# Thirteen of 31 back-substitution steps of the leaf inversions moved from GpSimd to VectorE

## The chip, the cores and the metric

One core of a Trainium2 chip runs the whole layer. The metric is the device time of one execution in microseconds (us). The kernel before takes 4035.48 us, the median of three runs (4032.93 to 4040.57). The engines are called as in the profile: PE (TensorE matmuls), PEld (its weight loads), DVE (VectorE), ACT (ScalarE), POOL (GpSimd) and SP (SyncE, whose queue issues all the DMAs).

## What is computed

An encoder layer over two sequences of 2048 and 256 tokens, 18 tiles of 128 tokens in all, in f32. A projection feeds two mixers side by side, a differential attention and a bidirectional RWKV7 recurrence; an output projection and a squared-ReLU MLP follow.

```python
z = jnp.einsum("bsd,dc->bsc", h, w_in)
o_da = diff_attn_mixer(z[..., :DA_COLS], ...)      # softmax(q k^T) of two halves, subtracted, times v
o_rw = rwkv7_mixer(z[..., DA_COLS:], ...)          # the scan below, in both directions
x = x + jnp.einsum("bsc,cd->bsd", mixed, w_out)
...
def step(state, inp):                               # rwkv7_scan, one token
    r_t, w_t, k_t, v_t, a_t, b_t = inp
    sa = jnp.einsum("dbhij,dbhj->dbhi", state, a_t)
    state = (state * w_t[..., None, :] + sa[..., :, None] * b_t[..., None, :]
             + v_t[..., :, None] * k_t[..., None, :])
    y = jnp.einsum("dbhij,dbhj->dbhi", state, r_t)
    return state, y
```

The kernel runs the scan in chunks of 64 tokens. Inside a chunk the recurrence is a triangular system of 64x64 for each head and direction, and its inverse is built from 32x32 diagonal blocks: each diagonal block is inverted by itself (the leaf), and a merge joins two of them.

## The kernel before, in words

Three stages follow one another: projection and preparation (to about 950 us of the trace), attention and recurrence together (about 950 to 2150 us), output projection and MLP (to the end).

In the middle stage the function `build` interleaves two streams of work in program order: `attn_stream`, which for each head and tile of 128 queries computes scores, exponentials and the product with the values, and `rw_units`, which goes through 18 units. A unit is one tile of the forward direction and one of the backward direction. For a unit numbered v the stream issues `rw_inter` for unit v+2 (products of the chunk, L933 to L942), `rw_leaf` for unit v+2, `rw_chain` for unit v (two chunks, one after the other, that carry the state S, L1043 to L1084) and `rw_merge` for unit v+1 (L973 to L1003). The order of the instructions on each engine is laid out when the kernel is built, by a planner that simulates a timeline and takes ready instructions by their place in the program; on the chip each engine then works through its own list in order.

The leaf works on 128 partitions that hold 64 diagonal blocks twice, each half for half of the columns. It loads the blocks (`lm`, L953, from the DRAM scratch MD that L942 writes) and the start value (`lx`, L954, unit columns), runs 31 back-substitution steps, and writes the result to the DRAM scratch XD (L963), from which the merge loads it (`xt`, L973). Each step is a multiply into `ltmp` and an add into `lx`; step i covers i rows and 16 - i // 2 columns. The tiles `lm`, `lx` and `ltmp` have one buffer each.

```python
for i in range(31, 0, -1):                                             # L955
    k0 = i // 2
    n = 16 - k0
    e = nc.vector if i >= LFV else nc.gpsimd                           # L958
    e.tensor_tensor(out=tmp[:, 0:i, 0:n], in0=lm[:, 0:i, i:i + 1].to_broadcast([128, i, n]),
                    in1=X[:, i:i + 1, k0:16].to_broadcast([128, i, n]), op=ALU.mult)
    e.tensor_tensor(out=X[:, 0:i, k0:16], in0=X[:, 0:i, k0:16], in1=tmp[:, 0:i, 0:n], op=ALU.add)
```

With LFV = 14 the steps 31 to 14 run on DVE and the steps 13 to 1 on POOL. In the same stage DVE also computes the row maxima of the attention scores (`nb`, L604, from PSUM), the sum of two exponential tiles (`P`, L639), the small combine steps (L617 to L626), the masks of the chunk products (L935) and the copies and state updates of the chain (L1043, L1044, L1051, L1072, L1073). POOL also copies `nat` into `tt` (L980) and computes small factors for the attention output (`ors`, L658 to L660). ACT takes the exponentials (L608, three score buffers `sc`), scales them (L631) and copies most PSUM results.

Of the kernel before, what the change touches and what calls it, by code (L numbers as in the profile page):

```python
# [57 lines left out]
class K:  # L58
# [886 lines left out]
    def rw_leaf(self, u):  # L945
# [9 lines left out]
# [5 lines that stand above are left out]
# [256 lines left out]
RUN0 = False  # L1216
HPS = ""
SCA = (0, 1, 2, 3)
LFV = 14
AT = 2  # L1220
XNB = 2
XTB = 2
# [94 lines left out]
```

## Time and profile before

| | |
|---|---|
| median of three runs | 4035.48 us (4032.93 to 4040.57) |
| the profiled execution | 4034.81 us, span of the trace 4032.6 us |
| busy over the span | PE 96%, DVE 61%, ACT 50%, POOL 14% |
| first and last leaf instruction | 996.2 us (DVE), 2087.4 us (POOL) |
| busy in the 1092 us from 996 to 2088 | PE 1045.54, DVE 844.41, ACT 832.67, POOL 322.12 us |

The shares over the whole span are an average over three stages; only the middle stage holds leaf work, so that its own stretch is the one to read. A group of instructions is listed with its line, its tiles (out<-in), its shape, its count, its busy time and mean duration, and the idle time of its engine just before it with what ended that.

### The profile page before, as it was taken

The numbers are of one execution on the slowest core, as the hardware profiler recorded it, in microseconds if no ns is written. First come the engines' busy times: TensorE is split into PE (matmuls) and PEld (weight loads), VectorE is DVE, ScalarE is ACT, GpSimd is POOL, SyncE is SP. The second block draws the span as 40 slices with busy tenths as digits, with TensorE's granted clock in tenths as the row PEclk, the third lists the DMA queues.
The fourth block names the chain that finished last, engine by engine and source line by source line (L and its number), as shares of the span: only waits on it lengthen the run. The fifth ranks groups of instructions, "written<-read, shape, count | busy, mean of one in ns | idle before, by whom it ended". The sixth has DMA issues, their size and how long they took to land.

```text
span 4032.6 us, 75020 instructions
## 1 busy us (share of the span) xinstructions
PE 3861.2 (96%) x28646; PEld 3444.1 (85%) x28646; DVE 2458.1 (61%) x5132; ACT 2033.0 (50%) x4652; POOL 568.6 (14%) x1062
## 2 busy tenths in 40 slices
PE   8999997887999999999998999999999999999999
PEld 7999997886787778777876889999999999999998
DVE  4245888866777878776875765444444444444443
ACT  4345666645777787777784234333333333333332
POOL 0000121111332223222323430000000000000000
PEclk9999997898999999999998999999999999999999
DMA  7566876774334435334324474222252222422221
GB/s 246 201 220 195 245 240 200 209 204 123 83 94 133 101 94 135 89 89 129 89 61 163 142 237 159 63 63 63 63 188 63 63 63 63 157 63 63 63 63 40
DMA packets 614583, 506.51 MB, mean 126 GB/s; under 512 B 250632, under 2 KB 543440, under 8 KB 607568
## 3 DMA queue, kind: packets, MB, share of 16 engines
q1 hardware_dynamic: 614224, 501.73, 42.2%
q8 instruction: 225, 3.69, 0.4%
q14 instruction: 134, 1.10, 0.1%
HBM read 336.41 MB, written 165.17 MB: 124 GB/s over the span
## 4 chain that ended last, share of the span: by engine, by line
PE 73%; DMA 9%; DVE 7%; ACT 5%; POOL 2%; SPq 2%; issue 2%; DVEq 0%; ACTq 0%; POOLq 0%
PE ups L100 7%; PE ups L101 7%; PE ups L102 7%; PE yps L102 7%; PE yps L101 7%; PE yps L100 7%; PE oo L650 4%; PE scp L933 3%; PE mm L100 3%; PE mm L102 3%; PE mm L101 3%; PE sc L601 2%; PE atp L645 2%; PE sc L602 2%; PE wops L100 2%
## 5 line engine op out<-in xcount | busy, mean ns | idle before, releaser
L517 DVE TENSOR_TENSOR acc<-yps,acc 128x512 f32<-128x512 f32 x576 | 392.0, 688 | 380.9 <-PE yps L102 380.9
L100 PE MATMUL ups<-h2hi,f_hi 128*128 128x384 f32 x1536 | 520.3, 339 | 0.0
L101 PE MATMUL ups<-h2lo,f_hi 128*128 128x384 f32 x1536 | 520.2, 339 | 0.0
L102 PE MATMUL ups<-h2hi,f_lo 128*128 128x384 f32 x1536 | 519.8, 338 | 0.0
L101 PE MATMUL yps<-f_lo,uh 128*128 128x512 f32 x1152 | 450.8, 392 | 0.0
L100 PE MATMUL yps<-f_hi,uh 128*128 128x512 f32 x1152 | 448.8, 390 | 0.0
L102 PE MATMUL yps<-f_hi,ul 128*128 128x512 f32 x1152 | 444.6, 393 | 0.0
L604 DVE TENSOR_REDUCE nb<-sc 128x1 f32<-128x512 f32 (+1 forms) x528 | 348.3, 676 | 130.8 <-PE sc L602 128.7
L137 ACT CAST f_hi<-f_raw 128x1024 fp32r<-128x1024 f32 x96 | 96.2, 1047 | 649.3 <-PE yps L102 647.6
L608 ACT ACTIVATE P<-sc,nb 128x512 f32<-128x512 f32 (+1 forms) x528 | 359.1, 684 | 82.6 <-DVE nb L604 80.0
L650 PE MATMUL oo<-vv,at 128*128 128x128 f32 x2080 | 303.9, 291 | 16.5 <-ACT at L647 13.4
L650 PEld LDWEIGHTS oo<-vv,at 128*128 128x128 f32 x2080 | 265.6, 198 | 40.9 <-ACT at L647 20.8
L505 DVE TENSOR_TENSOR ul<-u,uh 128x384 fp32r<-128x384 f32 x192 | 106.8, 556 | 307.4 <-ACT uh L504 303.7
L101 PEld LDWEIGHTS ups<-h2lo,f_hi 128*128 128x128 f32 x1536 | 288.2, 188 | 6.3
L100 PEld LDWEIGHTS ups<-h2hi,f_hi 128*128 128x128 f32 x1536 | 288.3, 188 | 5.9
L102 PEld LDWEIGHTS ups<-h2hi,f_lo 128*128 128x128 f32 x1536 | 288.2, 188 | 5.5
L100 PE MATMUL mm<-w_hi,hT_hi 128*128 128x256 f32 x864 | 259.8, 301 | 18.7 <-DVE qn L343 11.1
L601 PE MATMUL sc<-kt,qq 128*128 128x512 f32 (+1 forms) x528 | 246.1, 466 | 24.0 <-ACT P L608 17.0
L101 PE MATMUL mm<-w_lo,hT_hi 128*128 128x256 f32 x864 | 256.0, 297 | 0.2
L102 PEld LDWEIGHTS yps<-f_hi,ul 128*128 128x128 f32 x1152 | 216.1, 188 | 46.7
L102 PE MATMUL mm<-w_hi,hT_lo 128*128 128x256 f32 x864 | 255.5, 296 | 0.0
L142 ACT ACTIVATE f_hi<-f_raw,g 128x256 fp32r<-128x256 f32 x384 | 168.9, 500 | 171.2 <-PE ups L101 110.5
(237 smaller groups left out, 8713.2 us busy)
## 6 DMA issues: line engine op xcount, KB each, us to landing
f_raw<-w_ff SPq DMA_DIRECT2D x192, 256.0 KB, 2.9
f_raw<-w_ff SPq DMA_DIRECT2D x96, 512.0 KB, 4.4
AR<-aro SPq DMA_DIRECT2D x36, 512.0 KB, 3.9
qq<-QT SPq DMA_DIRECT2D x288, 64.0 KB, 2.4
ar<-AR SPq DMA_DIRECT2D x36, 512.0 KB, 4.9
bk<-BK SPq DMA_DIRECT2D x36, 512.0 KB, 3.8
ZT<-zs SPq DMA_DIRECT2D x84, 192.0 KB, 3.8
xt<-x SPq DMA_DIRECT2D x27, 512.0 KB, 4.5
```

Of the source, the lines that this page charges most:

```text
L100: mm(ps, lh, rh, start=start, stop=False)
L101: mm(ps, lh, rl, start=False, stop=False)
L102: mm(ps, ll, rh, start=False, stop=stop)
L137: nc.scalar.copy(hi[:, ks], raw)
L142: nc.scalar.activation(out=hi[:, k], in_=raw[:, k - k0], func=AF.Copy, scale=gk)
L505: nc.vector.tensor_tensor(out=ul[:, ns], in0=u2, in1=uh[:, ns].bitcast(F32), op=ALU.subtract)
L517: nc.vector.tensor_tensor(out=acc[j][:, cs], in0=ps, in1=acc[j][:, cs], op=ALU.add)
L601: nc.tensor.matmul(sc, qq[:, c, 0], kt, start=True, stop=False)
L604: nc.vector.tensor_reduce(out=m, in_=sc, axis=AX.X, op=ALU.max, negate=True)
L608: nc.scalar.activation(out=P, in_=sc, func=AF.Exp, bias=m, accum_out=(a["ls"][:, hf] if a["nh"] > 1 else a["l"])[:, c:c + 1])
L650: nc.tensor.matmul(a["op"], at[:, b], a["kv"][1][hf][:, b], start=k == 0, stop=k == a["n"] - 1)
L933: nc.tensor.matmul(ps[:, c], bk[hs, c, x].rearrange("p s t -> p (s t)"), ar[hs, c, x].rearrange("p s t -> p (s t)"), start=True, stop=True)
```

## The change

One constant is changed. It sets from which step on the leaf leaves DVE for POOL; with 1 all steps 31 to 1 run on DVE, and POOL has no leaf instruction left.

```diff
@@ -1216,7 +1216,7 @@
 RUN0 = False
 HPS = ""
 SCA = (0, 1, 2, 3)
-LFV = 14
+LFV = 1
 AT = 2
 XNB = 2
 XTB = 2
```

Per unit 26 instructions change their engine (13 multiplies, 13 adds), in 18 units 468. Nothing else in the program text differs, but the planner lays out all the lists of the program anew.

## Rows read from the trace of the kernel before

**Rows 1.** The page's busy times over the whole span: busy us, share of the span, instructions.

```profile
PE 3861.2 (96%) x28646; PEld 3444.1 (85%) x28646; DVE 2458.1 (61%) x5132; ACT 2033.0 (50%) x4652; POOL 568.6 (14%) x1062
```

**Rows 2.** Busy time of each engine in stretches of the middle stage (start:end, length, then busy us of each engine with instruction counts, granted TensorE clock, DMA share, GB/s): all the leaf work, then its first 400 us and the remainder.

```profile
996.00:2088.00 1092.00, 1045.54 (x12336) 862.85 (x12335) 844.41 (x2104) 832.67 (x2063) 322.12 (x821) 0.97 0.40 100
...
1000.00:1400.00 400.00, 375.44 (x4429) 314.67 (x4429) 307.51 (x793) 298.57 (x740) 120.30 (x309) 0.95 0.42 104
1400.00:2088.00 688.00, 666.10 (x7887) 544.75 (x7884) 533.17 (x1297) 531.41 (x1318) 201.55 (x511) 0.99 0.39 98
```

**Rows 3.** Groups of instructions of POOL in the stretch from 996 to 2088 us: the leaf's adds and multiplies.

```profile
L961 POOL TENSOR_TENSOR lx<-lx,ltmp 128x130 f32<-128x130 f32 (+12 forms) x234 | 94.0, 402 | 16.9
L959 POOL TENSOR_TENSOR ltmp<-lm,lx 128x130 f32<-128x130 f32 (+12 forms) x234 | 92.5, 395 | 39.0 <-DVE lx L961 22.6
```

**Rows 4.** Groups of DVE with different shapes kept apart, from 950 to 2260 us: leaf multiplies of shapes that the POOL steps have too, or nearly.

```profile
L959 DVE TENSOR_TENSOR ltmp<-lm,lx 128x133 f32<-128x133 f32 x18 | 5.2, 289 | 0.1
L959 DVE TENSOR_TENSOR ltmp<-lm,lx 128x110 f32<-128x110 f32 x18 | 5.0, 278 | 0.2
L959 DVE TENSOR_TENSOR ltmp<-lm,lx 128x120 f32<-128x120 f32 x18 | 5.0, 278 | 0.1
...
L959 DVE TENSOR_TENSOR ltmp<-lm,lx 128x96 f32<-128x96 f32 x18 | 4.5, 252 | 0.1
L959 DVE TENSOR_TENSOR ltmp<-lm,lx 128x78 f32<-128x78 f32 x18 | 4.4, 247 | 0.2
...
L959 DVE TENSOR_TENSOR ltmp<-lm,lx 128x56 f32<-128x56 f32 x18 | 4.1, 225 | 0.3
...
L959 DVE TENSOR_TENSOR ltmp<-lm,lx 128x30 f32<-128x30 f32 x18 | 3.9, 217 | 0.3
```

**Rows 5.** The groups of all DVE leaf instructions from 996 to 2088 us: adds and multiplies.

```profile
L961 DVE TENSOR_TENSOR lx<-lx,ltmp 128x31 f32<-128x31 f32 (+2 forms) x324 | 85.8, 265 | 4.5
L959 DVE TENSOR_TENSOR ltmp<-lm,lx 128x31 f32<-128x31 f32 (+2 forms) x324 | 85.7, 265 | 51.7 <-DMA lx<-eye 25.5 <-DMA lm<-MD 16.1 <-issue 3.9
```

**Rows 6.** Busy time in eight stretches in which POOL runs its 13 leaf steps, after 1470 us (columns as in rows 2; the first, the last, the sum).

```profile
1475.60:1488.20 12.60, 12.60 (x183) 10.36 (x178) 9.01 (x15) 9.78 (x26) 10.84 (x30) 1.00 0.20 51
...
2074.30:2087.60 13.30, 13.30 (x210) 10.79 (x210) 10.40 (x18) 12.37 (x32) 11.49 (x28) 1.00 0.21 50
sum 105.90, PE 105.90 PEld 87.08 DVE 83.23 ACT 86.26 POOL 90.12; mean PE 13.24 PEld 10.88 DVE 10.40 ACT 10.78 POOL 11.26
```

**Rows 7.** The same in six stretches in which DVE runs its 18 leaf steps.

```profile
1450.80:1472.60 21.80, 21.80 (x277) 18.17 (x278) 21.15 (x70) 18.85 (x47) 2.18 (x5) 1.00 0.36 104
...
2047.70:2074.20 26.50, 26.50 (x311) 21.28 (x310) 23.61 (x73) 20.55 (x53) 3.97 (x10) 1.00 0.17 46
sum 142.70, PE 138.26 PEld 114.56 DVE 133.13 ACT 106.90 POOL 20.05; mean PE 23.04 PEld 19.09 DVE 22.19 ACT 17.82 POOL 3.34
```

**Rows 8.** The same in seven stretches between two leaves, with no leaf step on either engine.

```profile
1488.20:1514.50 26.30, 25.58 (x276) 21.27 (x275) 19.20 (x41) 21.83 (x54) 3.35 (x8) 1.00 0.52 113
...
2018.70:2047.70 29.00, 27.59 (x283) 22.03 (x283) 20.90 (x45) 23.84 (x61) 3.03 (x9) 1.00 0.40 77
sum 202.30, PE 195.71 PEld 158.26 DVE 139.17 ACT 164.37 POOL 23.85; mean PE 27.96 PEld 22.61 DVE 19.88 ACT 23.48 POOL 3.41
```

**Rows 9.** Waits between 996 and 2088 us (who waited for whom: us in total, times, longest us).

```profile
ACT P L608 <- DVE nb L604: 68.9, 75, 5.2
...
ACT o L662 <- POOL ors L660: 13.6, 13, 2.8
...
PE sc L601 <- ACT P L608: 13.0, 9, 4.4
...
PE oo L650 <- ACT o L662: 1.7, 2, 0.9
```

**Rows 10.** The chain that ended last in the stretch from 1000 to 1400 us, by line.

```profile
by line: PE oo L650 13.3%; PE scp L933 12.1%; PE sc L601 6.9%; PE atp L645 6.2%; DMA XD<-lx 5.3%; PE sc L602 5.2%; POOL lx L961 4.5%; POOL ltmp L959 4.2%; ACT P L608 3.8%; issue 3.7%; PE bp L938 2.8%; DMA ar<-AR 2.4%; PE mp L987 2.1%; PE qp
```

**Rows 11.** SP's queue in order of time, first around 1150 us, then around 1560 us (start, us, queue, line, DMA, count): the write of a finished leaf, and the loads by its merge.

```profile
1148.62 2.60 SPq L963 DMA_DIRECT2D XD<-lx  x2
...
1154.58 0.36 SPq L954 DMA_DIRECT2D lx<-eye  x1
1154.99 2.78 SPq L973 DMA_DIRECT2D xt<-XD  x4
...
1551.76 1.95 SPq L963 DMA_DIRECT2D XD<-lx  x2
...
1569.80 2.06 SPq L973 DMA_DIRECT2D xt<-XD  x4
```

**Rows 12.** DVE in order of time inside one leaf (start, us, engine, line, instruction).

```profile
1453.52 0.23 DVE L959 TENSOR_TENSOR ltmp<-lm,lx 128x81 f32<-128x81 f32 x1
1453.79 0.24 DVE L961 TENSOR_TENSOR lx<-lx,ltmp 128x81 f32<-128x81 f32 x1
1454.07 0.24 DVE L959 TENSOR_TENSOR ltmp<-lm,lx 128x78 f32<-128x78 f32 x1
1454.34 0.24 DVE L961 TENSOR_TENSOR lx<-lx,ltmp 128x78 f32<-128x78 f32 x1
1454.50 0.69 DVE L604 TENSOR_REDUCE nb<-sc 128x1 f32<-128x512 f32 x1
1455.10 0.25 DVE L959 TENSOR_TENSOR ltmp<-lm,lx 128x100 f32<-128x100 f32 x1
```

**Rows 13.** Groups of DVE: the sum of two exponential tiles (both inputs in SBUF) in the stretch 2005.1:2018.7 (one of those of rows 6), in 1746.7:1779 (one of those of rows 8), and over 950 to 2260 us with shapes apart.

```profile
L639 DVE SCALAR_TENSOR_TENSOR P<-P,g,P 128x512 f32<-128x512 f32 x4 | 3.2, 848 | 0.0
...
L639 DVE SCALAR_TENSOR_TENSOR P<-P,g,P 128x512 f32<-128x512 f32 x8 | 5.7, 741 | 0.1
...
L639 DVE SCALAR_TENSOR_TENSOR P<-P,g,P 128x512 f32<-128x512 f32 x252 | 181.3, 765 | 2.9 <-ACT P L631 0.7
```

## The prediction

> **What bounds the kernel now.** I read the whole page first: PE is busy 96% of the span, DVE 61%, POOL 14% [rows 1]. That mean hides the stage that matters, so the next view is the busy time between 996 and 2088 us, where the leaf runs: PE 1045.54 of 1092 us, DVE 844.41 (77%), ACT 832.67 (76%), POOL 322.12 [rows 2]. PE is the bound there too, with 46 us of idle time, of which 25 us lie in the first 400 us, where the granted clock is also lower (0.95 against 0.99) [rows 2]. So what the change is worth is read from how long PE idles next to each kind of leaf work, and not from POOL's or DVE's busy time.
>
> The third view cuts the stage by what the leaf does. While POOL runs its 13 steps, PE is busy in all of 105.9 us and DVE in 83.23 (79%) [rows 6]. While DVE runs its 18 steps, DVE is busy in 133.13 of 142.7 us (93%) and PE in 138.26: 4.4 us idle, 3.1% [rows 7]. Between leaves DVE is at 69% and PE idles 6.6 of 202.3 us, 3.3% [rows 8]. The reader is to see that the POOL part is at present the one part of the unit in which PE never runs dry.
>
> **What leaves POOL.** 468 instructions with 94.0 + 92.5 = 186.5 us, 10.4 us per unit [rows 3]. None of that is PE's time. POOL's other work then no longer stands behind leaf steps: ACT waited 13.6 us for POOL's `ors`, and PE 1.7 us for what ACT did next [rows 9]. I book a gain of 1 us, between 0 and the 13.6.
>
> **What DVE takes on.** The 13 steps have 130, 120, 121, 110, 108, 96, 91, 78, 70, 56, 45, 30 and 16 elements. From the nearest DVE shapes [rows 4], 0.289 once, and two each of 0.278, 0.278, 0.252, 0.247, 0.225 and 0.217, gives 3.28 us for the multiplies; the adds cost the same (265 ns mean in both groups [rows 5]). That is 6.6 us per unit and 118 us in 18 units. DVE would stand at (844 + 118) / 1092 = 88%, still below PE: it doesn't become the bound by its sum.
>
> **What DVE gets back.** With POOL on the leaf, the sum of two tiles takes 848 ns on DVE, without it 741; over the stage the mean is 765, so 252 times 24 ns is 6 us [rows 13]. With the few other DVE instructions of the same kind I take 8 us in all, 0.4 us per unit, from the 118. The net load is 110 us, 6.1 per unit.
>
> The Trainium skill, page "SBUF — State Buffer", section "Who interferes with whom", says that a DVE instruction with two SBUF inputs and a GpSimd instruction that reads SBUF lock each other out, the later one blocking fully. That speaks for this change, and by it alone DVE could get back up to POOL's whole leaf time, 186 us, against 118 added, so DVE would end lighter and the terms below vanish. The trace agrees on the direction, with 848 against 741 ns [rows 13], and puts the size at a twentieth of that.
>
> **What lies on the path.** Three terms.
>
> First, the POOL part of a unit becomes more of the DVE part. A DVE step takes 142.7 / (6 x 18) = 1.32 us, since DVE alternates leaf instructions with others [rows 7, 12]; POOL's takes 105.9 / (8 x 13) = 1.02 [rows 6]. So 13.2 us with no PE idle become 17.2 us at 3.1%. The 4 extra us replace time between leaves, at 3.3%, and cost nothing. 13.2 x 3.1% is 0.41 us per unit, 7.4 us in all.
>
> Second, in those 13.2 us DVE has (105.9 - 83.2) / 8 = 2.8 us free [rows 6], and gets 6.1 more. 3.3 us per unit of its work, row maxima and sums among it, are done later, in a part where DVE is idle 31% [rows 8]. The trace of before shows no such backlog, so I bound it: 0, if the idle time takes all of it, and 18 x 3.3 = 59 us, if PE waits for all of it. Behind a late row maximum stands ACT's exponential (68.9 us of waits for L604 now), and behind that PE, which waits for a score buffer (13.0 us now) [rows 9]: about a fifth of ACT's wait reaches PE, and three score buffers take up the rest. I take a tenth, 6 us, since half of the late work is the leaf itself, which nobody awaits.
>
> Third, the leaf ends later by 4 us, or by up to 4 us earlier where the wait for the hand-over to POOL (22.6 us in all [rows 3]) falls away. After 1400 us this has a cover: the merge's load is issued 18 us after the leaf is written [rows 11], because it waits for the merge before. If that cover were gone the merge would be late, then the chain. Before 1400 us there is little: load of the next `lx`, then `xt`, 6.4 us behind the write in SP's queue [rows 11], and the POOL leaf stands on the chain that ended last with 8.7% of 400 us [rows 10]. What is late there is the recurrence, while attention fills PE; PE's idle share there is 6% [rows 2]. Seven units times 4 us at 6% is 1.7 us.
>
> No DMA is added or moved. The write of the leaf (L963) waits on DVE in place of POOL, and the score loads behind it in SP's queue wait with it; that is in the third term. No new wait stands on DVE: a step follows its predecessor on the same engine.
>
> Sum: 7.4 + 6 + 1.7 - 1 = 14 us. The profiled execution took 4034.81 us, 0.7 below the median of the three runs; 4034.8 + 14 = **4049 us**.
>
> **The rivals.** *The idle time takes it all.* DVE at 88% still has 130 us free, the leaf has nobody waiting for it after 1400 us, and PE's 3.1% in the DVE part might come from ACT and not from DVE, as the 3.3% without leaf work suggests [rows 7, 8]. Then the first two terms are nothing and the time is 4036 us, within 8 us of before. For it speaks that both idle shares agree; against it, that PE idles nothing in the POOL parts.
>
> *The leaf gets shorter, and the kernel faster.* A DVE step whose two instructions follow each other takes 0.54 us [rows 12] against POOL's 1.02. If the planner puts the last 13 steps back to back, the leaf ends 13 x 0.48 = 6 us earlier, plus 1.3 us for the hand-over. In the early units that stand on the chain [rows 10], the recurrence then gains 7 x 7 = 50 us of lead, and could feed PE where it idles: at most the 25 us in the first 400 us [rows 2]; I take half, 12 us, which gives 4022 us. It needs steps that aren't alternated with other work; the DVE steps of now mostly are.
>
> By the skill's rule above, with DVE lighter than before, the time would also come out here, at or below 4035 us; 24 ns against 741 [rows 13] leave that little weight, and its chance is in that of this rival.
>
> *DVE becomes what PE waits for.* From the point at which the work put off in one leaf isn't done before the next begins, PE waits for row maxima in every unit. 3.3 us put off meet 8.9 us of free DVE time between leaves (63 us in seven stretches [rows 8]), of which the longer leaf takes 4 us of length. The price is up to the 59 us above, with the first term 66, so about 4100 us at the end and 4075 in the middle. Against it speaks the margin.
>
> **How the numbers follow.** The forecast, a small loss of 5 to 25 us (4040 to 4060): 0.40. All absorbed, 4028 to 4043: 0.27. Faster, 4010 to 4027: 0.18. DVE as the bound, 4060 to 4100: 0.15. A measurement of this kernel can tell about 0.2%, 8 us, so same means 4027 to 4043.5. Faster is the third case, 0.18; same is the second and a little of the forecast, 0.32; slower is the remaining 0.50. The range leaves out the lower half of the third case and the upper third of the last: 4020 to 4085. The forecast's own range is 4040 to 4060.
>
> **What would show it.** In the changed trace L959 and L961 stand on DVE with 558 instructions each and together near 290 us (171.5 + 118), and on POOL with none. DVE is busy 945 to 965 us of the leaf's stretch. L639's mean falls from 765 to about 741. A leaf takes about 41 us from its first step to its last, in one alternating run on DVE. PE's idle time in the stage grows by 10 to 15 us, in the places where POOL worked, with DVE's L604 ahead of it in the waits. The first step is wrong if PE stays fully busy in the leaf's last 13 steps; the second if ACT's wait for L604 doesn't grow from 68.9 us; the third if merges after 1400 us wait for the leaf. The prediction as a whole is wrong if the planner lays out PE's list so differently that the stage moves by more than these terms, or if the time is below 4027 us.

## The result and the profile after

The changed kernel takes 4055.24 us, the median of six runs (4051.02 to 4065.62), against 4036.79 for the kernel before (six runs, 4022.96 to 4040.57): a ratio of 1.0053, 95% interval 1.0040 to 1.0066, that is 18.5 us slower by the medians and 21 by the ratio. The forecast was 14 us, 4049 us. The profiled execution of the changed kernel is the longest of its six (4065.62 us, 10 us over their median), so what its trace shows against [rows 1 to 13] adds up to 31 us and not to 18.5.

The page's busy times (as rows 1):

```profile
PE 3865.8 (95%) x28646; PEld 3459.5 (85%) x28646; DVE 2526.8 (62%) x5600; ACT 2036.5 (50%) x4652; POOL 389.8 (10%) x594
```

The same number of matmuls; 468 instructions have gone from POOL to DVE. The busy time by stretches (as rows 2); the fourth line goes from 950 us to the first matmul of the output projection:

```profile
996.00:2088.00 1092.00, 1033.40 (x12112) 865.62 (x12111) 887.86 (x2489) 822.47 (x2031) 146.21 (x346) 0.95 0.40 99
...
1000.00:1400.00 400.00, 371.52 (x4280) 314.85 (x4279) 329.27 (x935) 303.72 (x747) 53.56 (x129) 0.94 0.40 97
1400.00:2088.00 688.00, 657.88 (x7810) 547.34 (x7807) 556.99 (x1551) 515.28 (x1277) 92.65 (x217) 0.95 0.40 100
...
950.00:2198.90 1248.90, 1156.94 (x13606) 969.08 (x13605) 977.92 (x2721) 916.51 (x2260) 177.24 (x409) 0.94 0.41 101
```

For the last line the kernel before has this one:

```profile
950.00:2170.00 1220.00, 1149.01 (x13592) 949.65 (x13592) 909.78 (x2242) 912.57 (x2257) 344.35 (x873) 0.96 0.41 103
```

The stage is 28.9 us longer, which is nearly all of the 31 us. PE's idle time grew from 71.0 to 92.0 us, and its busy time for the same work by 7.9 us at a granted clock of 0.94 in place of 0.96. The loss lies after 1400 us more than before it: there the clock was 0.99 [rows 2] and is 0.95. The last copy of a chain product ends the recurrence; before and after (minimum, median, maximum ns, first and last start):

```profile
L1051 DVE COPY q<-qp x36: 649/682/693, 1075.7 to 2149.7; 128x512 f32<-128x512 f32 x36
```

```profile
L1051 DVE COPY q<-qp x36: 675/688/693, 1091.0 to 2185.8; 128x512 f32<-128x512 f32 x36
```

The recurrence starts 15 us later and ends 36 us later. In all 14 traces of this case the first matmul of the output projection follows the last of these copies after 13 to 23 us, so that the end of the recurrence dates the end of the stage.

**The leaf on DVE.** Groups of DVE from 996 to 2150 us (as rows 5), then the sum of two exponential tiles over 950 to 2260 us (as rows 13):

```profile
L959 DVE TENSOR_TENSOR ltmp<-lm,lx 128x126 f32<-128x126 f32 (+22 forms) x558 | 142.5, 255 | 58.2 <-DMA lx<-eye 34.0 <-DMA xt<-XD 16.2 <-DMA qq<-QT 2.3
L961 DVE TENSOR_TENSOR lx<-lx,ltmp 128x126 f32<-128x126 f32 (+22 forms) x558 | 142.4, 255 | 6.6 <-DVE l L621 0.2
```

```profile
L639 DVE SCALAR_TENSOR_TENSOR P<-P,g,P 128x512 f32<-128x512 f32 x252 | 180.0, 761 | 1.6 <-ACT P L631 0.7
```

The leaf's instructions add up to 284.9 us on DVE, 113 more than in [rows 5], but DVE's busy time in the stage grew by only 68 us (909.78 to 977.92 above) and between 996 and 2088 us by 43 (844.41 to 887.86, where 945 to 965 was forecast). Over the whole trace DVE's instructions last 118.7 us longer in sum and its busy time grew by 68.7: neighbouring instructions overlap in the records, and 50 us of what was added lies in such overlaps.

DVE in order of time: the first and last instruction of one leaf, and the first of the next (start, us; in brackets the idle time before and what ended it):

```profile
1494.69 0.21 DVE L959 TENSOR_TENSOR ltmp<-lm,lx 128x31 f32<-128x31 f32 x1 [3.79 <-DMA xt<-XD]
...
1548.45 0.18 DVE L961 TENSOR_TENSOR lx<-lx,ltmp 128x16 f32<-128x16 f32 x1
...
1562.71 0.21 DVE L959 TENSOR_TENSOR ltmp<-lm,lx 128x31 f32<-128x31 f32 x1 [4.15 <-DMA xt<-XD]
```

From the first start to the last this leaf takes 53.8 us, and the next begins 14.3 us later. Read so for all 18 units, the mean length is 52.8 us (before: 40.5), and 17 times out of 17 the next leaf follows after 9 to 15 us (before: 9 to 15 us behind the first seven leaves, 24 to 34 us from then on). From one leaf's start to the next it is 64.3 us in the mean, 61.8 before. SP's queue between these two leaves (as rows 11):

```profile
1549.75 3.77 SPq L963 DMA_DIRECT2D XD<-lx  x2
...
1558.70 0.53 SPq L954 DMA_DIRECT2D lx<-eye  x1
1559.28 2.36 SPq L973 DMA_DIRECT2D xt<-XD  x4
```

The one buffer of `lx` takes its new start value only after the write, and the first merge's load goes out 9.5 us after the write (5.9 to 11.0 in the later units), where before it went out 18 us after it in [rows 11] (8 to 28 in the later units): the merge now always waits for the leaf.

**Where PE idles.** The unit cut up as in rows 6 to 8, after 1400 us: sums over 11 stretches with the first 18 steps, 12 with the last 13 steps, 11 between leaves.

```profile
sum 377.75, PE 352.59 PEld 293.22 DVE 325.20 ACT 297.73 POOL 71.56; mean PE 32.05 PEld 26.66 DVE 29.56 ACT 27.07 POOL 6.51
...
sum 232.16, PE 228.19 PEld 189.48 DVE 211.25 ACT 180.06 POOL 19.85; mean PE 19.02 PEld 15.79 DVE 17.60 ACT 15.01 POOL 1.65
...
sum 129.77, PE 122.22 PEld 102.45 DVE 64.70 ACT 82.88 POOL 9.34; mean PE 11.11 PEld 9.31 DVE 5.88 ACT 7.53 POOL 0.85
```

PE is idle 6.7% of the first 18 steps (3.1% in [rows 7]), 1.7% of the last 13 (nothing in [rows 6]) and 5.8% between leaves (3.3% in [rows 8]); over all units after 1400 us, cut as here, the kernel before has 3.9, 0.9 and 3.8%. Over all 18 units, the first 18 steps and then the last 13, before:

```profile
sum 488.30, PE 463.02 PEld 383.09 DVE 443.25 ACT 373.15 POOL 79.76; mean PE 25.72 PEld 21.28 DVE 24.62 ACT 20.73 POOL 4.43
...
sum 245.60, PE 242.40 PEld 201.16 DVE 181.94 ACT 187.13 POOL 202.06; mean PE 13.47 PEld 11.18 DVE 10.11 ACT 10.40 POOL 11.23
```

And after:

```profile
sum 601.30, PE 558.52 PEld 467.18 DVE 514.74 ACT 471.01 POOL 108.04; mean PE 31.03 PEld 25.95 DVE 28.60 ACT 26.17 POOL 6.00
...
sum 353.00, PE 343.11 PEld 287.97 DVE 326.05 ACT 274.00 POOL 30.49; mean PE 19.06 PEld 16.00 DVE 18.11 ACT 15.22 POOL 1.69
```

PE's idle time in the last 13 steps grew by 6.7 us (3.2 to 9.9), and in the first 18 by 17.5 (25.3 to 42.8); between leaves it fell by 5.5 (18.0 to 12.5). So most of it came not where the steps came in but in the first part of the next leaf, where the merge now falls. One such place in four-microsecond windows, with PE's two waits in it and the two of ACT ahead of them:

```profile
1492.00:1496.00 4.00, 3.78 (x22) 2.73 (x21) 1.17 (x4) 0.00 (x0) 0.00 (x0) 1.00 0.71 171
1496.00:1500.00 4.00, 0.72 (x33) 0.62 (x33) 3.26 (x9) 1.64 (x6) 2.40 (x6) 0.91 0.40 108
1500.00:1504.00 4.00, 4.00 (x18) 3.88 (x18) 2.96 (x9) 3.93 (x10) 0.00 (x0) 0.50 0.30 75
...
1516.00:1520.00 4.00, 4.00 (x33) 3.61 (x32) 3.19 (x8) 1.39 (x5) 1.96 (x4) 0.96 0.73 231
```

```profile
1497.13 0.69 PE L987 MATMUL mp<-zt,sc 32*32 32x32 f32 x32 [1.35 <-DVE zt L981]
...
1499.97 2.07 PE L650 MATMUL oo<-vv,at 128*128 128x128 f32 x8 [2.14 <-ACT o L662]
```

```profile
1496.14 0.46 ACT L976 COPY nat<-xt 128x256 f32<-128x256 f32 x1 [5.22 <-DMA xt<-XD]
...
1499.55 0.37 ACT L662 ACTIVATE o<-oo,ors 128x128 f32<-128x128 f32 x1 [2.20 <-POOL ors L660]
```

ACT's list stands 5.22 us at the merge's copy `nat`, which waits for the load of the finished leaf. PE then waits for the merge's `zt` and for the attention output `o`, is busy 0.72 of 4 us, and runs fully busy at a granted clock of 0.50 (1.2 GHz) from 1500 until about 1516. Three microseconds of waiting cost more behind them, in a stretch that counts as busy. This is an example and not the sum: between 996 and 2100 us PE's waits for `zt` are 1.4 us in all and ACT's for `xt` no longer than before (46.3 us, before 49.3). What grew most is PE's wait for ACT's exponentials.

Waits from 996 to 2100 us (as rows 9):

```profile
ACT P L608 <- DVE nb L604: 67.9, 61, 4.2
ACT nat L976 <- DMA xt<-XD: 46.3, 18, 5.2
...
PE sc L601 <- ACT P L608: 22.5, 14, 3.8
```

In [rows 9] the first is 68.9 us and the last 13.0.

### The profile page after: what moved, and what is told of

It reads as the page before. It is cut to its first block, busy times and chain, and to the rows that moved or that the text cites. A ratio compares the mean times of both kernels' runs of the same rounds, so it can differ in the third digit from the quotient of the medians.

```text
span 4063.8 us, 74972 instructions
## 1 busy us (share of the span) xinstructions
PE 3865.8 (95%) x28646; PEld 3459.5 (85%) x28646; DVE 2526.8 (62%) x5600; ACT 2036.5 (50%) x4652; POOL 389.8 (10%) x594
## 5 line engine op out<-in xcount | busy, mean ns | idle before, releaser
L604 DVE TENSOR_REDUCE nb<-sc 128x1 f32<-128x512 f32 (+1 forms) x528 | 350.6, 677 | 105.5 <-PE sc L602 102.9
L650 PE MATMUL oo<-vv,at 128*128 128x128 f32 x2080 | 307.2, 293 | 24.4 <-ACT at L647 13.7
L143 DVE SCALAR_TENSOR_TENSOR f_lo<-f_raw,g,f_hi 128x256 fp32r<-128x256 f32 x384 | 168.7, 482 | 139.7 <-ACT f_hi L142 137.3
```

Source lines behind the costliest of these rows:

```text
L143: nc.vector.scalar_tensor_tensor(out=lo[:, k], in0=raw[:, k - k0], scalar=gk, in1=hi[:, k].bitcast(F32), op0=ALU.mult, op1=ALU.subtract)
L604: nc.vector.tensor_reduce(out=m, in_=sc, axis=AX.X, op=ALU.max, negate=True)
L650: nc.tensor.matmul(a["op"], at[:, b], a["kv"][1][hf][:, b], start=k == 0, stop=k == a["n"] - 1)
```

## The experiments

Three theories. **A, length:** the leaf, now 53 us with some 10 us of reload behind it, sets the pace of the recurrence. **B, load:** the 26 more instructions per unit hold up DVE's other work, whatever the leaf's length. **C, POOL:** what POOL loses gives time back, because its list is no longer held by leaf steps (C1) or because it no longer gets in DVE's way in SBUF (C2). Every kernel was timed in turn with the kernel before, whose median stands in brackets. Costs in us are ratios, or differences of ratios, times 4036, and their uncertainty is that of the two intervals together.

**Load without length.** The kernel before, with 26 further DVE instructions per unit of the shapes of steps 13 to 1. In the first kernel they read the leaf's own `lm` and `lx`:

```diff
+for i in range(13, 0, -1):
+    n = 16 - i // 2
+    nc.vector.tensor_tensor(out=self.dt[:, 0:i, 0:n], in0=lm[:, 0:i, i:i + 1]..., in1=X[:, 13:14, 8:9]..., op=ALU.mult)
+    nc.vector.tensor_tensor(out=self.dx[:, 0:i, 0:n], in0=self.dx[:, 0:i, 0:n], in1=self.dt[:, 0:i, 0:n], op=ALU.add)
```

> The kernel before, with the 26 DVE instructions of steps 13 to 1 added per unit on two tiles that nobody reads, while POOL still runs the real steps; the output is that of before. Theory A (the leaf's length: 53 us from first step to last in the changed trace against 41 before, and the next leaf can start only when the last one has been written): DVE gets the load but the leaf keeps its length, so 0 to 8 us slower than the kernel before. Theory B (the 118 us of DVE work make row maxima late and PE idle): the whole loss is here, 15 to 20 us slower.

4053.28 us [4036.28], ratio 1.0041 (1.0025 to 1.0057), leaf 41.2 us. But the gap between leaves grew to 15 to 21 us in the first ten units, since the added instructions keep `lm` and `lx` in use. The second kernel frees them: only the first added instruction reads the leaf, and the others use tiles of their own.

```diff
+    src = X[:, 13:14, 8:9] if i == 13 else self.dx[:, 0:1, 0:1]
+    nc.vector.tensor_tensor(out=self.dt[:, 0:i, 0:n], in0=self.dc[:, 0:i, 0:n], in1=src.to_broadcast([128, i, n]), op=ALU.mult)
+    nc.vector.tensor_tensor(out=self.dx[:, 0:i, 0:n], in0=self.dc[:, 0:i, 0:n], in1=self.dt[:, 0:i, 0:n], op=ALU.add)
```

> The kernel before with the 26 extra DVE instructions per unit on tiles of their own; unlike the first run of this kind they read neither lm nor, but once, lx, so that they can't hold the leaf's buffers. Theory A: 0 to 8 us slower than before, the first run's 17 us having come from buffers held. Theory B: 15 to 20 us slower again.

4051.61 us [4033.46], 1.0036 (1.0022 to 1.0050), leaf 41.7 us, gaps of 10 to 15 us in the first seven units and 18 to 35 us later, nearly as before. DVE's load alone costs 15 to 17 us (uncertainty 6) with the leaf's length nearly unchanged. B holds, and A alone doesn't explain the change. In the second kernel part of this price goes another way than in the changed kernel, where POOL has no leaf steps: POOL's `ors` [rows 9] comes later, ACT's wait for it grew from 13.6 to 35.4 us and PE's behind it from 1.7 to 11.6. In the changed kernel the two are 7.7 and 2.7 us.

**Two buffers for `lm`, `lx` and `ltmp`**, in the changed kernel and in the kernel before, so that a leaf can start while the last one is being written:

```diff
-        X = sp.tile([128, 32, 16], F32, name="lx", tag="lx", bufs=1)
+        X = sp.tile([128, 32, 16], F32, name="lx", tag="lx", bufs=2)
```

> The changed kernel with two buffers each for lm, lx and ltmp in place of one, so that a leaf may be loaded and begun before the previous one has been written. Theory A: most of the 18 us of loss goes, 4030 to 4042 us. Theory B: the DVE load is the same, 4050 to 4060 us.

> The kernel before with two buffers each for lm, lx and ltmp. Theory A: the early units, where one leaf follows straight on another, speed up, 4 to 12 us faster than before. Theory B: nothing changes on DVE, within 4 us of before. It is also the partner of the run with two buffers and all steps on DVE: the difference of the two is the price of the DVE load without the serial leaf, near 0 to 6 us under A, 15 or more under B.

The changed kernel: 4041.90 us [4036.28], 1.0015 (1.0004 to 1.0025). The leaf is still 51.5 us long, but the first two leaves and the fifth overlap with the next, the mean from one start to the next is 61.8 us again, and the recurrence ends where it did before:

```profile
L1051 DVE COPY q<-qp x36: 679/685/692, 1097.9 to 2151.6; 128x512 f32<-128x512 f32 x36
```

With all of DVE's load kept, 15 us of the 21 are gone (0.0015 in place of 0.0053, uncertainty 7 us): a long leaf costs where the next must wait for it. The kernel before: 4038.24 us [4036.28], 1.0007 (0.9997 to 1.0018); A's gain did not come, so at 40.5 us the wait for the buffers does not set the time. The two kernels with two buffers differ by 0.0008, 3 us with an uncertainty of 6, which is what A gave for the pair. That doesn't make the load free: the pair also differs by the POOL work that the changed kernel no longer has, and the runs below price it.

**Steps 13 to 1 left out**, then their load put back beside the leaf, on POOL or on DVE:

```diff
-        for i in range(31, 0, -1):
+        for i in range(31, 13, -1):
```

> The kernel before with the 13 POOL steps left out (steps 13 to 1 aren't computed at all, so the inverses are incomplete): the leaf is some 14 us shorter, DVE's list of work is as before. Theory A, if the leaf's length sets the pace of the recurrence in the kernel before too: 8 to 20 us faster than before. Theory B: POOL's work is off the path, within 4 us of before.

> The same 18-step leaf with the 26 instructions per unit on DVE instead: the DVE load of the change with a leaf 14 us shorter than that of before. Theory A: 4003 to 4012 us. Theory B (the DVE load is what costs): 4018 to 4025 us, 15 to 20 above the 18-step leaf.

> The 18-step leaf (steps 13 to 1 left out, as in the earlier run at 4003 us), and 26 POOL instructions of the shapes of the left-out steps per unit on tiles that nobody reads, begun when step 14 is done: POOL's load of before without its place in the leaf. Theory A (the leaf's length set the 33 us that leaving the steps out gained): 4003 to 4010 us. Theory C (POOL's leaf work itself slows DVE or holds POOL's other work): 4025 to 4036 us.

Without the steps 4002.84 us [4036.28], 0.9919 (0.9905 to 0.9934), 33 us, more than either theory gave. With the DVE load of the kernel above 4020.69 us [4033.46], 0.9964 (0.9947 to 0.9981). With the same instructions on POOL 4028.96 us [4033.46], 0.9985 (0.9970 to 0.9999). Beside the first, the DVE load costs 0.0045, 18 us with an uncertainty of 9, a third time about the same; and the POOL load costs 0.0066, 27 us with an uncertainty of 8, although nobody waits for it: C holds, and POOL's leaf work was far from free. With POOL's load kept, the shorter leaf by itself gained 6 us (0.9985, uncertainty 6). The kernel with the DVE load differs from the changed kernel only in that steps 13 to 1 are off the leaf's chain: 0.9964 against 1.0053, 36 us with an uncertainty of 9. That is A, at a leaf of 25.8 us in the one and 52.8 in the other.

**POOL held without reading SBUF.** The same short leaf, with one small POOL instruction that waits for the leaf and 25 memsets, to tell C1 from C2:

```diff
+        nc.gpsimd.tensor_tensor(out=self.dx[:, 0:1], in0=self.dc, in1=X[:, 13, 8:9], op=ALU.mult)
+        for i in range(25):
+            nc.gpsimd.memset(self.dx[:, 0:400], 0.0)
```

> The 18-step leaf (steps 13 to 1 left out) and, in place of the 26 POOL instructions with two inputs, one small POOL multiply and 25 POOL memsets of 128x400 per unit on a tile that nobody reads: POOL is held for about as long, but the memsets read nothing. Theory C1 (POOL's leaf work costs because its other work stands behind it in its list): about as slow as with the two-input instructions, 4020 to 4035 us. Theory C2 (it costs because two-input instructions on POOL and DVE hold each other): 4003 to 4012 us, as the 18-step leaf alone.

4022.26 us [4035.77], 0.9964 (0.9951 to 0.9976). Its memsets, and its sum of two exponential tiles:

```profile
L966 POOL MEMSET dx<- 128x400 f32 x450 | 196.4, 436 | 23.4
```

```profile
L639 DVE SCALAR_TENSOR_TENSOR P<-P,g,P 128x512 f32<-128x512 f32 x252 | 178.9, 754 | 4.5 <-ACT P L631 2.6
```

Holding POOL for 196 us costs 0.0045 beside the short leaf, 18 us, with DVE undisturbed (754 ns; 757 with no POOL load, 777 with the two-input load). So most of C is not C2: what two-input instructions add, 0.0021 or 8 us, is no larger than its uncertainty. That it is C1 is what remains of the two, and this trace does not show the wait that carries it: ACT's wait for POOL's `ors` is 11.4 us, with the short leaf alone 10.7.

**The whole leaf on POOL** (`LFV = 32`):

> The opposite change: all 31 steps on POOL (the constant at 32). DVE loses 171 us of work. A POOL step takes about 1 us, so the leaf would be near 33 us long against 41 before. Theory A: 5 to 20 us faster than before. Theory B, by DVE's load: 10 to 25 us faster too. Theory C: POOL's doubled leaf work holds its other work and DVE, no gain or slower.

4076.41 us [4033.46], 1.0104 (1.0079 to 1.0128), with the shortest leaf (34.7 us) and 127 us less of DVE (717.93 against 844.41 us from 996 to 2088). By A and by B it should have gained. Here the waits show C1:

```profile
ACT o L662 <- POOL ors L660: 78.2, 37, 4.5
...
PE oo L650 <- ACT o L662: 24.4, 17, 2.6
```

Against [rows 9], ACT waits 78.2 us in place of 13.6 for POOL's `ors`, behind leaf steps in POOL's list, and PE waits 24.4 in place of 1.7 us for ACT.

**A longer leaf without load.** The kernel before with three round trips of `lx` through DRAM between steps 14 and 13:

```diff
+            if i == 13:
+                for z in range(3):
+                    nc.sync.dma_start(out=self.LD[u % 4], in_=X)
+                    nc.sync.dma_start(out=X, in_=self.LD[u % 4])
```

> The kernel before with three round trips of lx to DRAM and back put between the last DVE step and the first POOL step, so that the leaf gets some 12 us longer and no engine but the DMA queue gets more work; results as before. Theory A (a leaf of 53 us and 10 us of reload set the pace of the recurrence): 15 to 30 us slower than before. Theory B (DVE's load is the whole loss): within 5 us of before.

4116.46 us [4035.77], 1.0193 (1.0169 to 1.0216). The leaf takes 57.5 us and the next follows after 9 to 12 us in all 17 cases; the reload stands behind the write as in the changed kernel:

```profile
1664.00 2.57 SPq L968 DMA_DIRECT2D XD<-lx  x2
...
1669.97 0.35 SPq L955 DMA_DIRECT2D lx<-eye  x1
...
1671.49 2.07 SPq L978 DMA_DIRECT2D xt<-XD  x4
```

```profile
996.00:2088.00 1092.00, 985.20 (x11577) 832.19 (x11578) 782.06 (x1962) 785.76 (x1936) 290.63 (x750) 0.94 0.46 120
```

78 us for 17 us per unit, 306 us in 18 units. That is far above the 15 to 30 us that A gave, and it came with a lighter DVE (782 us), so B does not hold here. But the run has not only the length: its round trips go through the one DMA queue and hold POOL's list, and two waits that are not the leaf's show it:

```profile
ACT o L662 <- POOL ors L660: 39.8, 23, 4.5
PE scp L934 <- DMA ar<-AR: 31.1, 11, 4.1
```

Before, they are 13.6 us [rows 9] and 3.7 us, and the DMA share is 0.46 against 0.40. How much of the 78 us is the length alone is not shown.

**Other splits** (`LFV = 8` and `LFV = 5`):

> The kernel before with the constant at 8: steps 13 to 8 move to DVE, 7 to 1 stay on POOL. By the prices of the runs so far (0.13 us of time for each us of POOL leaf work, 0.14 for each of DVE's) POOL's 98 us less give 13 us back and DVE's 59 us more cost 8; the leaf grows by 2 to 4 us to some 44 and stays below the pace at which one follows straight on another. Theory A, in which the loss comes when leaf and reload (10 us) exceed the 62 us per unit: 4026 to 4036 us. Theory B alone: 4040 to 4046 us.

> The kernel before with the constant at 5: steps 13 to 5 on DVE, 4 to 1 on POOL. It asks where between 8 (4025 us) and 1 (4055 us) the loss begins. Theory A: leaf near 47 us, with 10 us of reload still under the 62 us of a unit, so 4020 to 4032 us, no worse than at 8 by more than a few us, and the loss comes with the last four steps. Theory B (DVE's load alone, in proportion): from 4025 at 8 to 4055 at 1 the time rises with the work moved (59 us of DVE work more at 8, 84 at 5, 118 at 1), so near 4038 us.

`LFV = 8`: 4024.86 us [4035.77], 0.9978 (0.9967 to 0.9989), faster than both kernels, 1 us below A's range and far from B's; leaf 43.7 us. `LFV = 5`: 4052.98 us [4034.06], 1.0044 (1.0027 to 1.0061), leaf 47.0 us. Their stretches from 996 to 2088 us:

```profile
996.00:2088.00 1092.00, 1051.75 (x12433) 867.43 (x12432) 887.93 (x2340) 845.74 (x2089) 232.86 (x610) 0.98 0.41 101
```

```profile
996.00:2088.00 1092.00, 1027.35 (x12240) 854.08 (x12239) 885.52 (x2408) 827.97 (x2046) 183.48 (x488) 0.97 0.40 100
```

PE is busy 24 us less with six instructions per unit more on DVE. The second missed what either theory gave: leaves follow straight on only in its first 11 units, its twelfth leaf starts with that of `LFV = 8` (1644 and 1645 us), and it falls behind from there (1986 and 1969 us at the seventeenth), when a leaf has 17 us or more to spare.

## Why the prediction was right in its total and wrong in two of its terms

A small loss was forecast and came (14 and 18.5 us), but two terms were far too small and of opposite sign. That the total came out is luck: the two errors nearly cancel.

**DVE's load** (the first and the second term, 13 us together) was about right: 15, 17 and 18 us in three kernels that have it without a longer chain. The first term, 7.4 us of idle PE in the last 13 steps, came in its place: 6.7 us over all 18 units, though not from nothing, as the eight stretches of [rows 6] have it, but from 3.2. The second, 6 us, failed by its own mark: ACT's wait for L604 is 67.9 us and was 68.9, so it was not row maxima that came late. The end of its path did grow by about that much, PE's wait for ACT's exponentials from 13.0 to 22.5 us; what held ACT was not traced. The net load of 110 us was too large as busy time: 68 us, as much of the added work overlaps with its neighbours. (63 us in seven stretches is 9.0 and not 8.9 us each; nothing hangs on it.)

**The relief of POOL** (-1 us, between 0 and 13.6) was mis-sized: 18 to 27 us. I read it from the waits that name POOL as the last releaser [rows 9], 13.6 us at most. With the whole leaf on POOL the price shows in these waits (78.2 us); with the memsets, 18 us, it doesn't, and where it acts is open.

**The leaf's length** (the third term, 1.7 us) is the step that failed. I took 41 us for the leaf, since a DVE step of 1.32 us replaces one of 1.02. The last 13 steps took 19.3 us each time (232.16 / 12, after 1400 us), 1.49 us for a step, and the first 18 took 34 us for 24; the merge now falls into them. In all the leaf grew by 12.3 us (40.5 to 52.8) and not by 4. The bound that mattered was one that I had not formed: 53 us of leaf and 10 to 15 of reload are the whole 60 to 70 us of a unit, so that the cover of 18 us [rows 11] went down to the bare reload in every unit, and not by 4 us. I had named that ("merges after 1400 us wait for the leaf") as what would show the term wrong, and the merge's loads show it. The runs from the short leaf give 0.9919 for the kernel before without the steps, +18 us for the load, +36 us for a chain of 52.8 us. The first figure, -33 us, holds the relief of 18 to 27 us and 6 to 15 us for a chain that is shorter than 40.5. The length term is thus 36 less 6 to 15, some 20 to 30 us, and two buffers take back 15 of them. These parts come from one path of edits, so that they must add up along it; the independent support is the load on the kernel before and the two buffers, and of the long leaf only the direction.

**The rival of a shorter leaf** failed on its own condition: the steps alternate with other work. With it went what DVE was to get back: the sum of two tiles fell from 765 to 761 ns, with 741 forecast, 1 us in 252 instructions. The kernels of the short leaf have 777 ns beside two-input POOL work, 757 without POOL load and 754 beside memsets. The Trainium skill's page "SBUF — State Buffer", section "Who interferes with whom", says that a DVE instruction with two SBUF inputs contends with a GpSimd instruction that reads SBUF, not with one that only writes it. These three agree with it in direction; the size, 20 ns of 757, is small. Why the changed kernel has 761 and not 757 or less was not found.

**Open.** The planner lays out all lists anew for each of these kernels, so a difference between two of them also holds that. In order of start, 13,668 of PE's 28,646 matmuls stand at another place in the changed kernel than before. No run here has the new engine or length with the old lists, so the order as a cause of its own is not excluded. 14, 8, 5 and 1 steps as the split give ratios of 1, 0.9978, 1.0044 and 1.0053, and neither load nor length has a step of 27 us between 8 and 5. What it is there was not found, and it is as large as the terms above; the sizes given for them are sizes of whole kernels, not of single waits.

## What to carry to other kernels

Moving work from one engine to another has three prices: what the giver's in-order list no longer holds up, what the taker's list now holds up, and the new length of the dependent chain, counted with the reload of its single buffer and set against the period of the loop. Busy shares and named waits understated the first and the third here; a kernel that has one price without the others (the load beside the chain, the chain with two buffers, the work left out) shows each by itself. The best split found was between the two ends, at 8 (0.9978).

## What the runs showed of the hardware

POOL work that nobody reads cost 18 us of 4036 (uncertainty 8) when it was 196 us of memsets, with POOL busy 344 of the 1092 us from 996 to 2088. After 3.3 us in which PE did almost nothing, its next 16 us or so were granted 0.50 of the clock (1.2 GHz) with PE fully busy, so this idle time was dearer than it was long. And a dependent step of two DVE instructions of 0.17 to 0.29 us took 1.49 us of time: in 135 of 216 of the last steps an instruction of 0.6 us or more of another stream stood in between, as in these rows of the changed kernel. They also show the overlap in the records: the second instruction starts 0.08 us before the first one's end.

```profile
1506.64 0.69 DVE L935 TENSOR_TENSOR sc<-scp,mask 128x512 f32<-128x512 f32 x1 [1.07 <-PE scp L933]
1507.25 0.25 DVE L959 TENSOR_TENSOR ltmp<-lm,lx 128x96 f32<-128x96 f32 x1
1507.41 0.16 DVE L618 TENSOR_TENSOR cf<-mx,nb 128x8 f32<-128x8 f32 x1
1507.79 0.69 DVE L604 TENSOR_REDUCE nb<-sc 128x1 f32<-128x512 f32 x1 [0.22 <-PE sc L602]
1508.40 0.25 DVE L961 TENSOR_TENSOR lx<-lx,ltmp 128x96 f32<-128x96 f32 x1
```
